# Long convolutions of a Hyena layer: float32 operands in place of hi/lo splits, one matrix table, more buffers and a lag of three

## The chip, the cores and the metric

One NeuronCore of a Trainium2 chip runs the whole program. The metric is the device time of one execution in microseconds (us); the time of a kernel is the median of its runs.

## What is computed

The reference is a small diffusion backbone: two layers, width 1024, 1024 latent tokens (and 256 context tokens). Layer 0 mixes with an RG-LRU, layer 1 with a bidirectional Hyena operator of order 2; a squared-ReLU MLP follows each, a norm ends it. The change touches the two long convolutions of the Hyena operator alone:

```python
def long_conv(u, k_f, bias):
    L = u.shape[1]
    u32 = u.astype(jnp.float32)
    y = jnp.fft.irfft(jnp.fft.rfft(u32, n=2 * L, axis=1) * k_f, n=2 * L, axis=1)[:, :L]
    return (y + u32 * bias).astype(u.dtype)

def hyena_operator(u, p, conv_fn):
    ...
    v, x1, x2 = jnp.split(z, HYENA_ORDER + 1, axis=-1)
    k_f = hyena_filters(L, fw1, fb1, fw2, fb2, fw3, fb3, fw4, freq)
    v = x1 * long_conv(v, k_f[:, 0], skip[0])
    v = x2 * long_conv(v, k_f[:, 1], skip[1])
    return v @ w_out + b_out
```

Each convolution is a product of spectra over 2L = 2048 points. `x1` (in the code X1) and `x2` (the tensor x2d) are gates.

## The kernel before

The kernel computes the transforms as block transforms on TensorE. A convolution order `o` and a half `c` of the 1024 channels are one unit, (0,0), (0,1), (1,0), (1,1). A unit's data is `BIG[u]`, 128 partitions x 16 blocks x 512 channels of float32; block `f` is one group of frequencies. Four functions in `hyena` do the work.

- `s1(u, g)` (L815 to L826): the first half of the forward transform for group g. Two float32 matmuls with `m1` (L822), each evicted by ScalarE into a tile `e` (L824; three buffers), which a DMA scatters into eight partition rows of `BIG[u]` (L826, big<-e).
- `fstep(u, j)` (L936 to L974): one step for frequency block `f = FORD[j]`. A DMA fetches the filter's block `ft` (L940; three buffers), a float32 matmul with `m2f` transforms it (L947), ScalarE copies it to `kk` (L949). BIG's block is split into two float32r tiles: `ah`, a rounded copy on ScalarE (L943), and `al`, the rest (L944), on POOL in odd steps and on DVE in even ones. `mm3` multiplies as three float32r matmuls, hi x hi, lo x hi, hi x lo (L133 to L135), with `m2h` and `m2l`. Four products of 64 partitions each on DVE form the complex product of the spectra, t1 and t2 (L956 to L959), and a sum follows (L968 at the ends of a unit; L970 in the ten middle steps, which are split again into `yh`, L972, and `yl`, L974).
- `bstep(u, j, y)` (L976 to L983): the transform back of block f, by mm3 with `mih`, `mil` in the middle steps and by a float32 matmul with `mif` (L982) in the others; ScalarE evicts it into `BIG[u]` (L983).
- `s2p(u, g)` (L920 to L934): the second half of the way back. Two DMAs gather rows of BIG into tiles `e` (L927, e<-big; five buffers), two float32 matmuls with `md` (L928), then DVE multiplies by the gate X1 (L932) in order 0, or ScalarE copies (L934) in order 1.

The loop runs 64 fsteps, 16 a unit. Bstep i-LAG stands behind fstep i, with LAG 2. Between them stand side items, spread over steps 0 to 12 of unit 0 and LAG+1 to 12 of the others: eight s1 of unit 1 in unit 0; s2p of the unit before, then s1 of the unit after, in units 1 and 2; s2p of unit 2, then four `back` (transposes L999, gate by x2d L1000) in unit 3. So s2p(u-1) and s1(u+1) run beside the steps of u. Unit 3's own s2p come after the loop, inside the output projection. BIG of units 0 and 2 share one buffer, those of 1 and 3 another. PE's instructions keep program order in the loop (`pin`); the framework's scheduler places the others. The DMAs of s1, s2p and fstep are all issued on SyncE (SP). The tables m2h, m2l, mih and mil come over POOL's queue in pieces during unit 0, m2f and mif over SyncE's.

Of the kernel before, what the change touches and what calls it, by code (L numbers as in the profile page):

```python
# [16 lines left out]
P = 128  # L17
# [21 lines left out]
FORD = list(range(1, 9)) + [0] + list(range(9, 16))  # L39
# [7 lines left out]
def tile_block(ctx: ExitStack, tc: tile.TileContext, a, out, dbg=None):  # L47
    nc = tc.nc
# [74 lines left out]
    def pin(ins):  # L123

        if pinned[0]:
            if pinned[0] is not True:
                tc.add_manual_dep(ins.ins, pinned[0], NOSYNC, reason="order")
            pinned[0] = ins.ins.name
        return ins

    def mm3(ps, wh, wl, rh, rl, start, stop):

        first = pin(nc.tensor.matmul(ps, wh, rh, start=start, stop=False))  # L133
        pin(nc.tensor.matmul(ps, wh, rl, start=False, stop=False))  # L134
        pin(nc.tensor.matmul(ps, wl, rh, start=False, stop=stop))  # L135
        return first
# [652 lines left out]
    def hyena(load, xs, close_x, close_w, reopen_x, reopen_w):  # L789
        vst, bst = ExitStack(), ExitStack()  # L790
        units = [(0, 0), (0, 1), (1, 0), (1, 1)]
        cp = [None]
        with ExitStack() as st2:
# [21 lines left out]
            def s1(u, g):  # L815

                o, c = units[u]
                if g == 0 and u != 1:
                    BIG[u] = (cp[0] if u % 2 else xb).tile([P, 16, 512], F32, tag="big", name=nm("big"), bufs=1)
                for m in range(2):  # L820
                    ps = psum()
                    pin(nc.tensor.matmul(ps, m1[:, m], V[c][:, g], start=True, stop=True))  # L822
                    e = bp.tile([P, 512], F32, tag="e", name=nm("e"), bufs=3)
                    nc.scalar.copy(e, ps)  # L824
                    b = prow(2 * g + m)
                    nc.sync.dma_start(BIG[u][b:b + 29:4], e)  # L826
# [63 lines left out]
        with ExitStack() as st:  # L890
            cp[0] = bst.enter_context(tc.tile_pool(name="hd", bufs=1, side="right", reuse_waits="tile"))
            cA = st.enter_context(tc.tile_pool(name="hca", bufs=1, reuse_waits="tile"))
            cpool = st.enter_context(tc.tile_pool(name="hcb", bufs=1, reuse_waits="tile"))
            LAG = 2
            E2 = 5
            BIG[1] = cp[0].tile([P, 16, 512], F32, tag="big", name=nm("big"), bufs=1)
            m2 = {}
            for q in (0, 1, 3, 2):
                m2[q] = [cA.tile([P, 4, P], F32R, name=f"m2{n}{q}") for n in "hl"]

            for tag, dt, n in (("ah", F32R, 2), ("al", F32R, 2), ("kk", F32, 2), ("t1", F32, 2), ("t2", F32, 2), ("y", F32, LAG)):
                cpool.tile([P, 512], dt, tag=tag, name=nm(tag), bufs=n)
            mih = cpool.tile([P, 10, P], F32R, name="mih")
            mil = cpool.tile([P, 10, P], F32R, name="mil")
            mif = cpool.tile([P, 6, P], F32, name="mif")
# [8 lines left out]
            def load_mif(o):
                nc.sync.dma_start(mif[:, o:o + 3], a["mif"][:, o:o + 3])

            def load_mi(o):
                for t, n in ((mih, 0), (mil, 1)):
                    nc.gpsimd.dma_start(t[:, o:o + 5], a["mi"][n, :, o:o + 5])

            def s2p(u, g):
                o, c = units[u]
                po = psum()
                for m in range(2):
                    e = cp[0].tile([P, 512], F32, tag="e2", name=nm("e2"), bufs=E2)
                    b = prow(2 * g + m)
                    nc.sync.dma_start(e, BIG[u][b:b + 29:4])  # L927
                    pin(nc.tensor.matmul(po, md[:, m], e, start=(m == 0), stop=(m == 1)))  # L928
                if o == 0:
                    if g == 0:  # L930
                        V[c] = vtile()
                    nc.vector.tensor_tensor(V[c][:, g], po, X1[c][:, g], op=ALU.mult)  # L932
                else:
                    nc.scalar.copy(V[c][:, g], po)  # L934

            def fstep(u, j):  # L936
                o, c = units[u]
                f = FORD[j]
                ft = cA.tile([P, 512], F32, tag="ft", name=nm("ft"), bufs=3)
                nc.sync.dma_start(ft, fd[u, f])  # L940
                ah = cpool.tile([P, 512], F32R, tag="ah", name=nm("ah"), bufs=2)
                al = cpool.tile([P, 512], F32R, tag="al", name=nm("al"), bufs=2)
                nc.scalar.copy(ah, BIG[u][:, f])  # L943
                (nc.gpsimd if j % 2 else nc.vector).tensor_tensor(al, BIG[u][:, f], ah.bitcast(F32), op=ALU.subtract)  # L944

                pk = psum()
                pin(nc.tensor.matmul(pk, m2f[:, f], ft, start=True, stop=True))  # L947
                kk = cpool.tile([P, 512], F32, tag="kk", name=nm("kk"), bufs=2)
                nc.scalar.copy(kk, pk)  # L949

                ps = psum()
                mm3(ps, m2[j // 4][0][:, j % 4], m2[j // 4][1][:, j % 4], ah, al, True, True)
                t1 = cpool.tile([P, 512], F32, tag="t1", name=nm("t1"), bufs=2)
                t2 = cpool.tile([P, 512], F32, tag="t2", name=nm("t2"), bufs=2)
                lo, up = slice(0, 64), slice(64, 128)
                nc.vector.tensor_tensor(t1[lo], ps[lo], kk[up], op=ALU.mult)  # L956
                nc.vector.tensor_tensor(t1[up], ps[up], kk[up], op=ALU.mult)
                nc.vector.tensor_tensor(t2[lo], ps[up], kk[lo], op=ALU.mult)
                nc.vector.scalar_tensor_tensor(t2[up], ps[lo], -1.0, kk[lo], op0=ALU.mult, op1=ALU.mult)  # L959
                if f == 0:  # L960

                    nc.vector.tensor_copy(t1[64:65], t2[0:1])
                    nc.vector.memset(t2[0:1], 0.0)
                    nc.vector.memset(t2[64:65], 0.0)
                mid = 3 <= j < 13
                y = cpool.tile([P, 512], F32R if mid else F32, tag="y", name=nm("y"), bufs=LAG)
                if not mid:
                    nc.vector.tensor_tensor(y, t1, t2, op=ALU.add)  # L968
                    return y, None
                nc.vector.tensor_tensor(t1, t1, t2, op=ALU.add)  # L970
                yh = cpool.tile([P, 512], F32R, tag="yh", name=nm("yh"), bufs=LAG)
                nc.scalar.copy(yh, t1)  # L972
                yl = y
                (nc.gpsimd if j % 2 else nc.vector).tensor_tensor(yl, t1, yh.bitcast(F32), op=ALU.subtract)  # L974
                return yh, yl

            def bstep(u, j, y):
                ps = psum()
                if y[1] is not None:
                    mm3(ps, mih[:, j - 3], mil[:, j - 3], y[0], y[1], True, True)  # L980
                else:
# [10 lines left out]
            def back(ct):  # L992
# [3 lines left out]
                for g4 in range(2):  # L996
# [227 lines left out]
def _consts():  # L1224
# [164 lines left out]
```

## Time and profile before

| | us |
|---|---|
| median of 3 runs (2871.66 to 2874.5) | 2873.65 |
| the profiled execution, its own time | 2870.54 |
| its span in the trace | 2868.8 |
| PE busy in the span | 2680.0 |
| DVE busy | 1605.5 |
| ACT busy | 1098.6 |
| POOL busy | 245.2 |
| the loop of the block transforms, 1682.68 to 2032.40 | 349.72 |

Busy times are sums over one engine's instructions; engines run beside each other, so they do not add up. The loop begins with the first matmul of L947 and ends with the last eviction at L983. Its frequency steps can be told apart by the matmuls of L947: steps 0, 16, 32, 48 begin at 1682.7, 1749.4, 1837.1 and 1942.5 us, which are the ends of the units below. A float32 matmul leaves two records in the trace. In the rows of windows stand begin and end, the length, the busy time of each engine with its count of records, the granted clock, the busy share of the DMA engines and their rate. PEclk is the granted clock of TensorE as a share of its upper level.

### The profile page before, as it was taken

The page shows a single profiled execution, that of the slowest core. Times are in us where ns is not written, and L with a number is a line of the kernel's source. Part 1 is how long each engine was busy: PE and PEld are TensorE (multiplying, and loading weights), DVE is VectorE, ACT ScalarE, POOL GpSimd, SP SyncE. Part 2 cuts the span into 40 slices and gives each one's busy share as a digit, 9 for nine tenths or more (in the row PEclk, how much of TensorE's full clock was granted, in tenths as well). Part 3 has the DMA queues.
Part 4 walks back from the last instruction along what each step waited for, and adds up shares of the span by engine and source line. Part 5 has one row for each costly group of instructions (what it writes and reads, how often), then busy time and mean ns, then how long its engine had stood idle before and what let it go on. Part 6 is the DMA issues. An engine that isn't in the chain of part 4 may idle for free.

```text
span 2868.8 us, 29759 instructions
## 1 busy us (share of the span) xinstructions
PE 2680.0 (93%) x11298; PEld 2071.4 (72%) x11298; DVE 1605.5 (56%) x2193; ACT 1098.6 (38%) x1670; POOL 245.2 (9%) x154
## 2 busy tenths in 40 slices
PE   6789889999999999999999997778799999999998
PEld 1677777788777777788787763334488888888887
DVE  7666575875555555444833368768576333333336
ACT  6457667542333233322522244444434211122213
POOL 0223432100000000000100021112001000000000
PEclk8799999999999999999999999998899999999999
DMA  8431123344444434322313254455321111111112
GB/s 304 125 111 44 52 66 121 102 145 133 121 114 138 122 114 138 100 68 63 123 52 118 67 159 122 134 159 169 120 87 45 52 52 44 52 44 52 51 46 96
DMA packets 121794, 288.60 MB, mean 101 GB/s; under 512 B 11883, under 2 KB 28269, under 8 KB 121395
## 3 DMA queue, kind: packets, MB, share of 16 engines
q1 hardware_dynamic: 116578, 275.42, 31.6%
q0 software_dynamic: 3344, 9.18, 1.0%
q10 hardware_dynamic: 1728, 2.10, 0.2%
q8 instruction: 89, 1.46, 0.2%
q14 instruction: 55, 0.44, 0.0%
HBM read 215.08 MB, written 37.75 MB: 88 GB/s over the span
## 4 chain that ended last, share of the span: by engine, by line
PE 72%; DVE 11%; DMA 9%; ACT 6%; issue 2%; SPq 0%; POOL 0%; DVEq 0%; ACTq 0%; POOLq 0%
PE ps L152 52%; PE ps L134 4%; PE ps L133 4%; PE ps L135 4%; DMA e<-big 3%; DMA adaw<-in_ada_w_dram 2%; PE ps L396 2%; PE ps L928 1%; DVE xc L485 1%; DMA big<-e 1%; DMA eraw<-in_ada_w_dram 1%; DVE hf L588 1%; PE ps L822 1%; PE ps L947 1%; ACT r L525 1%
## 5 line engine op out<-in xcount | busy, mean ns | idle before, releaser
L152 PE MATMUL ps<-u,whi 128*128 128x512 f32 x2696 | 734.7, 394 | 0.0
L113 ACT CAST whi<-raw 128x1024 fp32r<-128x1024 f32 x206 | 216.3, 1050 | 1113.5 <-PE ps L152 1007.4
L152 PEld LDWEIGHTS ps<-u,whi 128*128 128x128 f32 x2696 | 505.1, 188 | 113.5 <-issue 7.4
L115 DVE TENSOR_TENSOR wlo<-raw,whi 128x1024 fp32r<-128x1024 f32 x206 | 261.9, 1271 | 467.8 <-ACT whi L113 467.0
L152 PE MATMUL ps<-u,wlo 128*128 128x512 f32 x1348 | 418.9, 390 | 0.0
L152 PE MATMUL ps<-hh,whi 128*128 128x512 f32 x896 | 296.7, 409 | 0.0
L152 PEld LDWEIGHTS ps<-u,wlo 128*128 128x128 f32 x1348 | 253.1, 188 | 53.0 <-DVE wlo L115 0.7
L152 PE MATMUL ps<-hh,wlo 128*128 128x512 f32 x896 | 282.1, 390 | 0.0
L152 PE MATMUL ps<-hl,whi 128*128 128x512 f32 x896 | 280.5, 390 | 0.0
L152 PEld LDWEIGHTS ps<-hh,whi 128*128 128x128 f32 x896 | 168.4, 188 | 51.3 <-issue 17.3
L134 PE MATMUL ps<-u,whi 128*128 128x512 f32 (+1 forms) x508 | 195.2, 385 | 3.5 <-POOL u L260 2.9
L133 PE MATMUL ps<-u,whi 128*128 128x512 f32 (+1 forms) x508 | 186.9, 385 | 11.5 <-ACT u L259 11.5
L745 DVE SCALAR_TENSOR_TENSOR big<-ps,mod,big 128x512 f32<-128x512 f32 (+1 forms) x132 | 91.7, 731 | 185.3 <-PE ps L152 177.7
L135 PE MATMUL ps<-u,wlo 128*128 128x512 f32 (+1 forms) x508 | 193.0, 382 | 1.8 <-DVE wlo L115 1.8
L152 PEld LDWEIGHTS ps<-hl,whi 128*128 128x128 f32 x896 | 168.3, 188 | 36.1 <-issue 1.0
L152 PEld LDWEIGHTS ps<-hh,wlo 128*128 128x128 f32 x896 | 168.2, 188 | 34.9
L745 DVE SCALAR_TENSOR_TENSOR x<-ps,mod,x 128x512 f32<-128x512 f32 x128 | 91.3, 746 | 145.1 <-PE ps L152 137.2
L195 DVE SCALAR_TENSOR_TENSOR acc<-adaw,cond,acc 128x512 f32<-128x512 f32 x98 | 73.6, 751 | 93.1 <-DMA adaw<-in_ada_w_dram 92.2
L260 POOL TENSOR_TENSOR u<-nu,u 128x512 fp32r<-128x512 f32 x24 | 33.9, 1413 | 1021.8 <-ACT u L259 1012.6
L133 PEld LDWEIGHTS ps<-u,whi 128*128 128x128 f32 x508 | 97.8, 193 | 29.9 <-ACT u L259 12.2
L134 PEld LDWEIGHTS ps<-u,whi 128*128 128x128 f32 x508 | 97.9, 193 | 25.4 <-POOL u L260 6.0
L135 PEld LDWEIGHTS ps<-u,wlo 128*128 128x128 f32 x508 | 97.4, 192 | 20.1 <-DVE wlo L115 3.0
(242 smaller groups left out, 4051.2 us busy)
## 6 DMA issues: line engine op xcount, KB each, us to landing
raw<-in_mlp_w_dram SPq DMA_DIRECT2D x136, 512.0 KB
adaw<-in_ada_w_dram SPq DMA_DIRECT2D x112, 256.0 KB
fd<-fe SPq DMA_DIRECT2D x64, 256.0 KB
big<-e SPq DMA_DIRECT2D x64, 256.0 KB
ft<-fd SPq DMA_DIRECT2D x64, 256.0 KB
e<-big SPq DMA_DIRECT2D x64, 256.0 KB
eraw<-in_ada_w_dram SPq DMA_DIRECT2D x24, 512.0 KB
raw<-in_hy_w_in_dram SPq DMA_DIRECT2D x24, 512.0 KB
```

The costliest lines, as they stand in the source:

```text
L113: lsplit[0] = nc.scalar.copy(hi, raw)
L115: lsplit[1] = nc.vector.tensor_tensor(lo, raw, hi.bitcast(F32), op=ALU.subtract)
L133: first = pin(nc.tensor.matmul(ps, wh, rh, start=start, stop=False))
L134: pin(nc.tensor.matmul(ps, wh, rl, start=False, stop=False))
L135: pin(nc.tensor.matmul(ps, wl, rh, start=False, stop=stop))
L152: nc.tensor.matmul(pp[c], x, y[c][k], start=first, stop=last)
L195: nc.vector.scalar_tensor_tensor(acc, w, s, acc, op0=ALU.mult, op1=ALU.add)
L260: applied[k % 2] = (nc.vector if k % 2 else nc.gpsimd).tensor_tensor(ul[k], u, uh[k].bitcast(F32), op=ALU.subtract)
L396: nc.tensor.matmul(p2, mf[:, 1 if g == 0 else 0], st.pop(("ht", i)), start=True, stop=True)
L485: eng.scalar_tensor_tensor(ov[:, :, so], zv[:, :, si], vcol("lru_conv_w", 8 * tap_ + dt), ov[:, :, so], op0=ALU.mult, op1=ALU.add)
L525: ins = nc.scalar.activation(*args, **kw)
L745: nc.vector.scalar_tensor_tensor(xs[m][:, cs], ps[:, :n], g2[:, m:m + 1], xs[m][:, cs], op0=ALU.mult, op1=ALU.add)
```

## The change

In the loop all operands are float32, and nothing is split. A step is one matmul for the filter, one for the signal and one back. One table `m2` (4 pieces of 128 x 4 x 192, whose columns 0 to 127 transform the signal and 64 to 191 the filter) and one table `mi` (4 pieces of 128 x 4 x 128) take the place of m2h, m2l, m2f, mih, mil and mif; all pieces come over POOL's queue. The sum y stands on GpSimd in all 64 steps. The DMA big<-e is issued on ScalarE for the units in the loop. Buffers: ft 3 to 8, e of s2p 5 to 6, kk, t1 and t2 2 to 3, y 2 to 4; LAG 2 to 3, so side items of units 1 to 3 begin a step later too. Nothing moves before the loop or after the beginning of the output projection.

```diff
@@ s1
-                    nc.sync.dma_start(BIG[u][b:b + 29:4], e)
+                    (nc.scalar if cp[0] else nc.sync).dma_start(BIG[u][b:b + 29:4], e)
@@ pools and tables
-            LAG = 2
-            E2 = 5
+            LAG = 3
...
+            m2 = [cA.tile([P, 4, 192], F32, name=f"m2{q}") for q in range(4)]
+            mi = [cA.tile([P, 4, P], F32, name=f"mi{q}") for q in range(4)]
+            for tag, n in (("kk", 3), ("t1", 3), ("t2", 3), ("y", LAG + 1)):
+                cpool.tile([P, 512], F32, tag=tag, name=nm(tag), bufs=n)
...
-            nc.sync.dma_start(m2f, a["m2f"])
...
             def load_m2(q):
-                for n in range(2):
-                    nc.gpsimd.dma_start(m2[q][n], a["m2w"][n, :, 4 * q:4 * q + 4])
+                nc.gpsimd.dma_start(m2[q], a["m2"][:, 4 * q:4 * q + 4])
...
+            def load_mi(q):
+                nc.gpsimd.dma_start(mi[q], a["mi"][:, 4 * q:4 * q + 4])
@@ s2p
-                    e = cp[0].tile([P, 512], F32, tag="e2", name=nm("e2"), bufs=E2)
+                    e = cp[0].tile([P, 512], F32, tag="e2", name=nm("e2"), bufs=6)
@@ fstep
-                ft = cA.tile([P, 512], F32, tag="ft", name=nm("ft"), bufs=3)
+                ft = cA.tile([P, 512], F32, tag="ft", name=nm("ft"), bufs=8)
                 nc.sync.dma_start(ft, fd[u, f])
-                ah = cpool.tile([P, 512], F32R, tag="ah", name=nm("ah"), bufs=2)
-                al = cpool.tile([P, 512], F32R, tag="al", name=nm("al"), bufs=2)
-                nc.scalar.copy(ah, BIG[u][:, f])
-                (nc.gpsimd if j % 2 else nc.vector).tensor_tensor(al, BIG[u][:, f], ah.bitcast(F32), op=ALU.subtract)
+                w = m2[j // 4][:, j % 4]
                 pk = psum()
-                pin(nc.tensor.matmul(pk, m2f[:, f], ft, start=True, stop=True))
+                pin(nc.tensor.matmul(pk, w[:, 64:192], ft, start=True, stop=True))
...
-                mm3(ps, m2[j // 4][0][:, j % 4], m2[j // 4][1][:, j % 4], ah, al, True, True)
+                pin(nc.tensor.matmul(ps, w[:, 0:128], BIG[u][:, f], start=True, stop=True))
...
-                mid = 3 <= j < 13
...
-                nc.vector.tensor_tensor(t1, t1, t2, op=ALU.add)
-                yh = cpool.tile([P, 512], F32R, tag="yh", name=nm("yh"), bufs=LAG)
-                nc.scalar.copy(yh, t1)
-                yl = y
-                (nc.gpsimd if j % 2 else nc.vector).tensor_tensor(yl, t1, yh.bitcast(F32), op=ALU.subtract)
-                return yh, yl
+                y = cpool.tile([P, 512], F32, tag="y", name=nm("y"), bufs=LAG + 1)
+                nc.gpsimd.tensor_tensor(y, t1, t2, op=ALU.add)
+                return y
@@ bstep
-                if y[1] is not None:
-                    mm3(ps, mih[:, j - 3], mil[:, j - 3], y[0], y[1], True, True)
-                else:
-                    pin(nc.tensor.matmul(ps, mif[:, j if j < 3 else j - 10], y[0], start=True, stop=True))
+                pin(nc.tensor.matmul(ps, mi[j // 4][:, j % 4], y, start=True, stop=True))
@@ before the loop
             load_m2(0)
-            late = {1: lambda: load_mif(0), 2: lambda: (nc.sync.dma_start(md, a["md"]), load_m2(1)), 3: lambda: load_mi(0),
-                    6: lambda: (load_m2(2), load_mi(5)), 9: lambda: (load_m2(3), load_mif(3))}
+            nc.sync.dma_start(md, a["md"])
+            load_mi(0)
+            late = {1: lambda: load_m2(1), 3: lambda: load_mi(1), 5: lambda: load_m2(2), 7: lambda: load_mi(2),
+                    9: lambda: load_m2(3), 11: lambda: load_mi(3)}
```

In what order the queues stand is seen at three places. SyncE's queue in unit 1, at the beginning of its s2p items, where it issues ft (the filter's blocks) and e (rows of BIG for s2p). Before:

```order
L940 DMA ft_12668<-fd 128x512
L927 DMA e_2436_12649<-big_10982 128x1x512
L927 DMA e_2437_12652<-big_10982 128x1x512
L927 DMA e_2440_12658<-big_10982 128x1x512
L927 DMA e_2441_12661<-big_10982 128x1x512
L927 DMA e_2454_12694<-big_10982 128x1x512
L940 DMA ft_12712<-fd 128x512
L940 DMA ft_12750<-fd 128x512
L927 DMA e_2455_12697<-big_10982 128x1x512
L927 DMA e_2457_12702<-big_10982 128x1x512
L927 DMA e_2458_12705<-big_10982 128x1x512
```

After the change, the same place:

```order
L928 DMA ft_12675<-fd 128x512
L915 DMA e_2390_12479<-big_10982 128x1x512
L915 DMA e_2391_12482<-big_10982 128x1x512
L915 DMA e_2394_12488<-big_10982 128x1x512
L915 DMA e_2395_12491<-big_10982 128x1x512
L915 DMA e_2405_12515<-big_10982 128x1x512
L915 DMA e_2406_12518<-big_10982 128x1x512
L928 DMA ft_12714<-fd 128x512
L928 DMA ft_12753<-fd 128x512
L915 DMA e_2408_12523<-big_10982 128x1x512
L915 DMA e_2409_12526<-big_10982 128x1x512
```

Six tiles e stand ahead of the next ft instead of five, the ft run further ahead of their steps, and no big<-e stands in this queue.

ScalarE's queue in unit 1, where its s1 items begin: e is s1's eviction, kk the filter's, big<-ps the eviction of a bstep, ah and yh the rounded copies. Before:

```order
L824 COPY e_12865<-ps_12863 128x512
L824 COPY e_12870<-ps_12868 128x512
L824 COPY e_12875<-ps_12873 128x512
L824 COPY e_12880<-ps_12878 128x512
L983 COPY big_11985<-ps_12883 128x512
L949 COPY kk_12896<-ps_12894 128x512
L972 CAST yh_12859<-t_2511_12848 128x512
L943 CAST ah_12980<-big_11985 128x512
L824 COPY e_12915<-ps_12913 128x512
L824 COPY e_12920<-ps_12918 128x512
L824 COPY e_12925<-ps_12923 128x512
L824 COPY e_12930<-ps_12928 128x512
```

After the change:

```order
L934 COPY kk_12679<-ps_12677 128x512
L824 COPY e_12693<-ps_12691 128x512
L826 DMA big_12622<-e_12693 8x16x512
L824 COPY e_12698<-ps_12696 128x512
L824 COPY e_12703<-ps_12701 128x512
L826 DMA big_12622<-e_12698 8x16x512
L826 DMA big_12622<-e_12703 8x16x512
L824 COPY e_12708<-ps_12706 128x512
L957 COPY big_11985<-ps_12711 128x512
L826 DMA big_12622<-e_12708 8x16x512
L934 COPY kk_12718<-ps_12716 128x512
L824 COPY e_12732<-ps_12730 128x512
```

The rounded copies are gone; the DMAs of big<-e stand among the copies, each behind the copy of its e, and some of them with the next copy ahead.

TensorE's queue, the last plain steps of unit 0. Before, with L947 the filter, L133 to L135 with ah and al the signal, the same lines with yh and y the block back in a middle step, and L982 the block back in another:

```order
L947 MATMUL ps_12502<-ft_12496,m2f 128x512
L133 MATMUL ps_12506<-ah_12498,m2h_11990 128x512
L134 MATMUL ps_12506<-al_12499,m2h_11990 128x512
L135 MATMUL ps_12506<-ah_12498,m2l_11991 128x512
L133 MATMUL ps_12518<-yh_12461,mih 128x512
L134 MATMUL ps_12518<-y_12459,mih 128x512
L135 MATMUL ps_12518<-yh_12461,mil 128x512
L947 MATMUL ps_12529<-ft_12523,m2f 128x512
L133 MATMUL ps_12533<-ah_12525,m2h_11990 128x512
L134 MATMUL ps_12533<-al_12526,m2h_11990 128x512
L135 MATMUL ps_12533<-ah_12525,m2l_11991 128x512
L982 MATMUL ps_12545<-y_12489,mif 128x512
```

After the change, with L932 the filter, L937 the signal and L956 the block back:

```order
L932 MATMUL ps_12350<-ft_12348,m_11989 128x512
L937 MATMUL ps_12354<-big_10982,m_11989 128x512
L956 MATMUL ps_12364<-y_12295,mi_11992 128x512
L932 MATMUL ps_12369<-ft_12367,m_11989 128x512
L937 MATMUL ps_12373<-big_10982,m_11989 128x512
L956 MATMUL ps_12383<-y_12324,mi_11993 128x512
L932 MATMUL ps_12388<-ft_12386,m_11986 128x512
L937 MATMUL ps_12392<-big_11985,m_11986 128x512
L956 MATMUL ps_12402<-y_12343,mi_11993 128x512
```

The five or seven matmul instructions of a step became three, all of float32, and the block that goes back is one step older.

## Rows read from the trace of the kernel before

**Rows 1.** The page, part 1: busy us of each engine (share of the span, instructions).

```profile
PE 2680.0 (93%) x11298; PEld 2071.4 (72%) x11298; DVE 1605.5 (56%) x2193; ACT 1098.6 (38%) x1670; POOL 245.2 (9%) x154
```

**Rows 2.** Windows by unit, then the loop: PE, PEld, DVE, ACT, POOL busy, PEclk, DMA, GB/s.

```profile
1682.68:1749.30 66.62, 55.23 (x150) 29.19 (x151) 63.00 (x94) 41.08 (x74) 19.33 (x18) 0.95 0.59 177
1749.30:1837.05 87.75, 72.36 (x187) 35.08 (x186) 67.61 (x101) 40.10 (x75) 16.93 (x13) 0.96 0.53 144
1837.05:1942.45 105.40, 79.75 (x187) 37.68 (x186) 74.91 (x110) 41.08 (x75) 17.17 (x14) 0.89 0.53 142
1942.45:2032.40 89.95, 66.72 (x191) 35.07 (x189) 76.40 (x108) 38.64 (x67) 16.63 (x13) 0.90 0.44 132
1682.68:2032.40 349.72, 274.06 (x712) 137.01 (x712) 281.92 (x410) 160.90 (x289) 70.05 (x57) 0.92 0.52 146
```

**Rows 3.** Windows: s2p of unit 1, its s1, s2p of unit 2, the slowest 20 us.

```profile
1760.90:1796.20 35.30, 30.02 (x71) 14.12 (x70) 26.13 (x40) 10.73 (x19) 6.35 (x5) 0.90 0.59 151
1796.20:1829.30 33.10, 29.39 (x82) 14.29 (x80) 23.70 (x36) 19.19 (x37) 6.73 (x5) 1.00 0.50 144
1852.10:1897.90 45.80, 33.12 (x72) 14.81 (x71) 26.45 (x41) 10.82 (x19) 6.34 (x5) 0.85 0.66 165
1860.00:1880.00 20.00, 14.74 (x26) 5.93 (x26) 7.78 (x12) 4.51 (x8) 1.69 (x2) 0.74 0.75 192
```

**Rows 4.** Groups of instructions in the loop: busy us, mean ns, then idle before and releasers.

```profile
L928 PE MATMUL ps<-e,md 128*128 128x512 f32 x96 | 53.9, 669 | 22.7 <-DMA e<-big 22.6
...
L957 DVE TENSOR_TENSOR t<-ps,kk 64x512 f32<-64x512 f32 x64 | 44.4, 694 | 0.9
...
L944 POOL TENSOR_TENSOR al<-big,ah 128x512 fp32r<-128x512 f32 x32 | 41.9, 1311 | 167.3 <-ACT ah L943 163.3 <-DMA ft<-fd 4.0
L943 ACT CAST ah<-big 128x512 fp32r<-128x512 f32 x64 | 40.0, 627 | 11.2 <-PE ps L135 5.0 <-DMA big<-e 4.6
...
L970 DVE TENSOR_TENSOR t<-t,t 128x512 f32<-128x512 f32 x40 | 30.5, 765 | 0.3
L982 PE MATMUL ps<-y,mif 128*128 128x512 f32 x48 | 29.4, 703 | 18.7 <-DVE y L968 17.1 <-ACT e L824 0.8 <-ACT ah L943 0.8
L824 ACT COPY e<-ps 128x512 f32<-128x512 f32 x48 | 27.9, 590 | 27.3 <-DMA big<-e 24.9 <-PE ps L822 2.1
...
L972 ACT CAST yh<-t 128x512 fp32r<-128x512 f32 x40 | 24.8, 622 | 19.5 <-DVE t L970 19.4
L944 DVE TENSOR_TENSOR al<-big,ah 128x512 fp32r<-128x512 f32 x32 | 24.1, 753 | 2.1 <-ACT ah L943 1.5
...
L968 DVE TENSOR_TENSOR y<-t,t 128x512 f32<-128x512 f32 x24 | 16.4, 688 | 0.5
L974 DVE TENSOR_TENSOR y<-t,yh 128x512 fp32r<-128x512 f32 x20 | 14.6, 729 | 6.9 <-ACT yh L972 4.2 <-PE ps L947 2.2
...
L999 PE MATMUL ps<-ident,v 128*128 128x128 f32 x32 | 4.4, 274 | 0.0
```

**Rows 5.** SyncE's queue in the loop, waits: us in total, times, longest.

```profile
SPq L940 <- PE ps L947: 98.4, 36, 8.1
SPq L826 <- ACT e L824: 37.7, 23, 4.0
```

**Rows 6.** The chain, 1795 to 1812 us: start us, length us, what (x records).

```profile
1796.37 0.86 PE ps L947 x2
1797.22 0.23 PE ps L133
...
1797.92 3.43 PE ps L822 x8
...
1807.01 4.40 DMA big<-e
```

**Rows 7.** Instructions on tile e, 1682 to 2040 us: ns min/median/max, first and last start.

```profile
L826 SPq DMA_DIRECT2D big<-e x48: 608/614/660, 1688.3 to 1930.0; - x48
```

**Rows 8.** Instructions of L1217, output at the end: ns min/median/max.

```profile
L1217 ACTq DMA_DIRECT2D out_dram<-o x12: 338/338/374, 2846.4 to 2865.6; - x12
```

More of the change, by code (lines that the diff above doesn't have):

```diff
@@ L893, in hyena @@
             cpool = st.enter_context(tc.tile_pool(name="hcb", bufs=1, reuse_waits="tile"))
-            LAG = 2
-            E2 = 5
+            LAG = 3
             BIG[1] = cp[0].tile([P, 16, 512], F32, tag="big", name=nm("big"), bufs=1)
[L897 to L905, printed above, removed]
+            m2 = [cA.tile([P, 4, 192], F32, name=f"m2{q}") for q in range(4)]
+            mi = [cA.tile([P, 4, P], F32, name=f"mi{q}") for q in range(4)]
+            for tag, n in (("kk", 3), ("t1", 3), ("t2", 3), ("y", LAG + 1)):
+                cpool.tile([P, 512], F32, tag=tag, name=nm(tag), bufs=n)
             md = cp[0].tile([P, 2, P], F32, name="md")
-            m2f = cA.tile([P, 16, P], F32, name="m2f")
-            nc.sync.dma_start(m2f, a["m2f"])
             def load_m2(q):
-                for n in range(2):
-                    nc.gpsimd.dma_start(m2[q][n], a["m2w"][n, :, 4 * q:4 * q + 4])
[L914 to L919, printed above, removed]
+                nc.gpsimd.dma_start(m2[q], a["m2"][:, 4 * q:4 * q + 4])
+            def load_mi(q):
+                nc.gpsimd.dma_start(mi[q], a["mi"][:, 4 * q:4 * q + 4])
             def s2p(u, g):
@@ L938, in fstep @@
                 f = FORD[j]
-                ft = cA.tile([P, 512], F32, tag="ft", name=nm("ft"), bufs=3)
+                ft = cA.tile([P, 512], F32, tag="ft", name=nm("ft"), bufs=8)
                 nc.sync.dma_start(ft, fd[u, f])
-                ah = cpool.tile([P, 512], F32R, tag="ah", name=nm("ah"), bufs=2)
-                al = cpool.tile([P, 512], F32R, tag="al", name=nm("al"), bufs=2)
-                nc.scalar.copy(ah, BIG[u][:, f])
-                (nc.gpsimd if j % 2 else nc.vector).tensor_tensor(al, BIG[u][:, f], ah.bitcast(F32), op=ALU.subtract)
+                w = m2[j // 4][:, j % 4]
                 pk = psum()
-                pin(nc.tensor.matmul(pk, m2f[:, f], ft, start=True, stop=True))
-                kk = cpool.tile([P, 512], F32, tag="kk", name=nm("kk"), bufs=2)
+                pin(nc.tensor.matmul(pk, w[:, 64:192], ft, start=True, stop=True))
+                kk = cpool.tile([P, 512], F32, tag="kk", name=nm("kk"), bufs=3)
                 nc.scalar.copy(kk, pk)
                 ps = psum()
-                mm3(ps, m2[j // 4][0][:, j % 4], m2[j // 4][1][:, j % 4], ah, al, True, True)
-                t1 = cpool.tile([P, 512], F32, tag="t1", name=nm("t1"), bufs=2)
-                t2 = cpool.tile([P, 512], F32, tag="t2", name=nm("t2"), bufs=2)
+                pin(nc.tensor.matmul(ps, w[:, 0:128], BIG[u][:, f], start=True, stop=True))
+                t1 = cpool.tile([P, 512], F32, tag="t1", name=nm("t1"), bufs=3)
+                t2 = cpool.tile([P, 512], F32, tag="t2", name=nm("t2"), bufs=3)
                 lo, up = slice(0, 64), slice(64, 128)
@@ L964, in fstep @@
                     nc.vector.memset(t2[64:65], 0.0)
-                mid = 3 <= j < 13
[L966 to L969, printed above, removed]
-                nc.vector.tensor_tensor(t1, t1, t2, op=ALU.add)
-                yh = cpool.tile([P, 512], F32R, tag="yh", name=nm("yh"), bufs=LAG)
-                nc.scalar.copy(yh, t1)
-                yl = y
-                (nc.gpsimd if j % 2 else nc.vector).tensor_tensor(yl, t1, yh.bitcast(F32), op=ALU.subtract)
-                return yh, yl
+                y = cpool.tile([P, 512], F32, tag="y", name=nm("y"), bufs=LAG + 1)
+                nc.gpsimd.tensor_tensor(y, t1, t2, op=ALU.add)
+                return y
             def bstep(u, j, y):
                 ps = psum()
-                if y[1] is not None:
-                    mm3(ps, mih[:, j - 3], mil[:, j - 3], y[0], y[1], True, True)
-                else:
-                    pin(nc.tensor.matmul(ps, mif[:, j if j < 3 else j - 10], y[0], start=True, stop=True))
+                pin(nc.tensor.matmul(ps, mi[j // 4][:, j % 4], y, start=True, stop=True))
                 nc.scalar.copy(BIG[u][:, FORD[j]], ps)
@@ L1281, in _consts @@
     mf[1, 0, 16, 0, :] = c1_[0]
-    def two(m):
-        hi = (m.view(np.int32) & np.int32(-4096)).view(np.float32)
-        return np.stack([hi, m - hi], 0)
     def lay(m, w=P):
@@ L1303, in _consts @@
     decay = np.ascontiguousarray(np.broadcast_to(-deltas, (P, D)))
-    return dict(m1=lay(m1), md=lay(md), mf=lay(mf), m2w=two(lay(m2[FORD][:, :, :P])), m2f=lay(m2[:, :, 64:]), mi=two(lay(mi[FORD[3:13]])), mif=lay(mi[FORD[:3] + FORD[13:]]), pos=pos2, tpos=tpos, decay=decay)
+    return dict(m1=lay(m1), md=lay(md), mf=lay(mf), m2=lay(m2[FORD], 192), mi=lay(mi[FORD]), pos=pos2, tpos=tpos, decay=decay)
 def _layout(i):
```

## The prediction

> **What bounds the kernel now.** Start with the page: TensorE (PE) is busy 93% of the span [rows 1]. That is a mean. Outside the block transforms its matmuls stand shoulder to shoulder and the change touches nothing, so the loop must be read alone: 1682.68 to 2032.40 us, 349.72 us, PE busy 274.06, VectorE (DVE) 281.92, ScalarE (ACT) 160.90, GpSimd (POOL) 70.05, DMA share 0.52 [rows 2]. No engine is full; the limit alternates. In unit 0 DVE is busy 63.00 of 66.62 us [rows 2]. Units 1 to 3 take 87.75, 105.40 and 89.95 us with neither PE nor DVE full [rows 2]. There two stretches must be told apart. While the s2p items run (e comes back from BIG, matmul, DVE or ACT), five or six frequency steps take 35.30 and 45.80 us; PE is busy 30.02 and 33.12 of it, at a granted clock of 0.90 and 0.85 of the upper level, 2.4 GHz [rows 3]. While the s1 items run, 33.10 us, PE 29.39 [rows 3].
>
> What do those stretches wait for? The engines' rows: PE idles 22.7 us before L928 and almost all of it is for DMA e<-big; ACT idles 27.3 before the e copy, 24.9 of it for DMA big<-e [rows 4]. The queue that issues these transfers says why they are late: SyncE stood 98.4 us in 36 waits at L940 (next ft) for the PE matmul that frees one of three ft buffers, 37.7 at L826 for ACT's e [rows 5]; e<-big stands behind both in program order.
>
> **The sum, part by part.** What PE does is priced from the chain at full clock: one float32 matmul (two records, L947) 0.86 us, eight records of L822 3.43, a split product 3 x 0.23 = 0.69 (L133, and the same for L134 and L135) [rows 6].
> - *PE.* 64 products and 40 middle back transforms go from 0.69 to 0.86: 104 x 0.17 = **+17.7 us** of PE work. After: 3 x 64 in steps, 96 in s1 and s2p, 288 x 0.86 = 247.7, and 4.4 for back's transposes (L999 [rows 4]): 252 us, the floor of the loop if nothing ever waits.
> - *DVE.* Leave: al 24.1, sums 30.5 and 16.4, yl 14.6 = **85.6 us** [rows 4]. Stay: four products of some 690 ns a step (L957 694; 64 x 2.77 = 177), s2p's and back's work. DVE comes to some 197 us and is full nowhere but in plain steps.
> - *ACT.* Leave 64 ah (40.0) and 40 yh (24.8) [rows 4]; come 48 issues of big<-e. One cost 614 ns on SyncE [rows 7]; ACT's nearest issue is that of the output, 338 [rows 8]. 48 of them are 16 to 29 us; I take 25 (the same transfer, so nearer the first). They lie on the ACT queue behind the e copy, with kk and the evictions behind them.
> - *POOL.* al and yl leave, 64 sums come, at 1311 ns (the same shape and two SBUF operands, L944) 84 us [rows 4]. A step of 2.9 us covers 1.3. Lag three gives a sum two whole steps before its back transform asks; before, L982 stood 17.1 us for DVE's sum [rows 4]. Should the cover fail, each step would grow by the 0.6 us by which POOL is slower.
> - *Tables.* One m2 and one mi, 2.5 MB by their tile shapes, take the place of 4.7. The first step's matmuls now both wait for m2's first quarter, 384 KB, where the first matmul of before used m2f, which had been loaded earlier on SyncE; I put 1.5 us there, between 0 and 4.40, the landing time of a 256 KB transfer [rows 6].
>
> Plain step, without a side item: PE 3 x 0.86 = 2.58, DVE 4 x 0.69 + gaps = 2.86; DVE sets it. Unit 0 shows what DVE's old five or six instructions cost: 66.62/16 = 4.2 us a step [rows 2].
>
> *Unit 0:* 8 steps carry one s1 (2.58 + 2 x 0.86 = 4.30 PE) and 8 do not. Bound 34.4 + 22.9 = 57.3; with the start and the e buffers (three, filled again only when big<-e has landed, 4.40 us [rows 6]) 60.5. **Gain 6.**
>
> *Units 1 and 2:* four steps carry two s2p each: PE 2.58 + 4 x 0.86 = 6.02. Four tiles e a step then come from DMA; before, 16 took about 35 us with five buffers, that is 2.2 each, with ft's waits in the queue. With the waits gone (eight ft buffers) and six in flight I take 1.5 to 1.6, so 6.3 us a step, 25 in all, against 35.30. Four or five steps carry two s1: PE again 6.02, but three e buffers recirculate in (0.59 + 4.40 + issue 0.3)/3 = 1.76 us, so 7 us for four e; 28.5 in all, against 33.10. Seven plain steps: 20.0. Unit 1 is 73.5 (before 87.75), **gain 14**; unit 2 has 2 MB of v<-x2d in the queue of its s2p items, 5 to 6 us more: 79.5 (105.40), **gain 26**.
>
> *Unit 3:* s2p 25 and some 2 of lead, four steps with back items 17, seven plain steps, 20, end of the pipe and big<-xd's start 8: 72 (89.95), **gain 18**.
>
> Sum of gains 64. From this I take 3 for half-clock stretches: the loop's mean clock is 0.92 [rows 2], and a loop with less idle should lose fewer, not more, but PE's float32 work lasts twice as long there. And 1 for the end, where the last sum now takes POOL's 1.3 us and not DVE's 0.69. Net **-60**. The profiled execution took 2870.54, so 2810.5; the median of the runs, 2873.65, is 3 us above it, and against that my figure is **2813 us**.
>
> One more thing on the queue that changes. What the move of big<-e takes off SyncE is 48 x 0.61 = 29 us of issuing and the 37.7 us of standing for e [rows 5, 7]; my s1 stretch stays held by three buffers and 4.40 us, with 28.5 us. If the other queue also made the transfer itself quicker, say 3 us, four e would take 4 x 1.3 = 5.2 us, PE's 6.02 would set the step, and three units would gain some 8 us more. The Trainium skill, in Trainium Kernel Development and Optimization, section Key Constraints, says that DMAs of all issuing queues run on the same 16 DMA engines, and that several queues save issue time only. By that rule the 8 us do not come; no row here has such a transfer on another queue.
>
> **Rivals.**
> 1. *Transfers keep their pace.* If e<-big is slow because of the DMA engines and not because SyncE stood at ft, the s2p stretches stay near 35 and 46 us and the s1 stretch near 33; only the plain steps and unit 0 gain. For: DMA share 0.59 and 0.66 in the s2p windows [rows 3]. Against: 98.4 us of waits ahead of them in the queue [rows 5]. Price: of the 60, 10 in each of units 1 and 3, 15 in unit 2, and 2 x 4.5 for s1 fall away: gain 16, 2858.
> 2. *PE alone sets the pace.* Buffers and lag cover everything: 252 plus about 12 for start, end and half clock: loop 264, gain 86, 2787. DVE's 2.86 against PE's 2.58 in some 30 plain steps (8 us) speaks against the very end.
> 3. *Half clock (the slower side).* Matmul work at full clock is 252 us. If 35 us of waiting stay, the loop is no shorter than 349.7 once 252/c = 315, a mean clock c of 0.80; the loop now has 0.92, an s2p stretch 0.85 [rows 2, 3]. At 0.74 throughout, the level of the slowest 20 us [rows 3], 252/0.74 + 35 = 375: 2899. Float32 throughout is what makes the clock dear: every wait in an s2p item that drops the clock then doubles 6.02 us of work. The Trainium skill, in TensorE: Matmul & The Clock Gate, section HAM oscillation, tells of a kernel whose matmul bursts fall back to the low clock at each DMA wait; the 0.85 stretch agrees in kind. Against: the s1 stretch has 1.00 [rows 3].
> 4. *ACT chains.* The change does not do what its queue move says: an e copy that waits for its buffer holds kk, the eviction and now the next big<-e itself, all on ACT. Then s1 stretches take 8 us a step instead of 7, three units, 2 x 4.5 + 4: 13 us less gain, 2825.
> 5. *POOL's sums slow DVE's products.* Sums on DVE took 765 ns in the middle steps, while POOL worked, and 688 at the ends of a unit, where it did not [rows 4]. If that ratio, 1.11, falls on the products, a plain step grows to 3.15, 30 of them by 9 us, and the start of the DVE-heavy unit 0 with them: 12 us, 2824. Against: L957, a product, has 694 in the same loop. GPSIMD Engine Reference, section 8 Key points, in the Trainium skill, says that GpSimd shares its SBUF interfaces with VectorE and contends with instructions that have two SBUF inputs; its section 4.1 would keep an add of two tiles on VectorE, as about twice as fast. The trace agrees with both (1311 against 688). A product here has one SBUF input, so by the first the 12 us do not come; by the second, with the sums left on DVE, 0.69 more in each of 30 plain steps would cost 21.
>
> **How the numbers follow.** Forecast as summed 0.47 (2798 to 2828 by the bounds: e<-big 1.3 to 1.9 us each, 48 x 0.3 to either side; issue 16 to 29; start 0 to 4); rival 2 0.16; rival 4 0.14; rival 1 0.12; rival 5 0.08; rival 3 0.03. The range that holds 8 in 10 takes in 4, 5 and the upper part of 2: **2788 to 2842**. What a measurement can tell from no change is 0.2%, 5.7 us; only rival 3 ends above it, and 0.02 is for rival 1 with a low clock on top: faster 0.95, same 0.02, slower 0.03.
>
> **What would show it.** Right: per step one pair at each of the three matmul lines and no split line in the loop; DVE's four product lines unchanged near 690 ns and its busy time near 200; plain steps of 2.8 to 3.0 us; the 98.4 us of ft waits on SyncE gone; POOL near 84 us, with no PE wait for y beyond unit ends; s2p stretches of 25 to 28 us. Wrong: L956's counterpart on PE waiting for POOL's y; products well above 700 ns while POOL adds (sharing of SBUF); s2p stretches still near 35 us with DMA e<-big as releaser (rival 1); granted clock under 0.85 over the loop (rival 3); ACT's e copy with more than the 24.9 us before (rival 4).

## The result and the profile after

The changed kernel takes 2836.32 us in the median (2834.56 to 2838.23, four runs), the kernel before 2873.03: a ratio of 0.9873, 95% interval 0.9859 to 0.9888, faster by 36.7 us. The profiled execution is that of 2838.23 us, with a span of 2836.4. Of the 32.4 us between the two spans, 32.0 are the loop's: 317.73 us now, 349.72 before [rows 2].

The page of the changed kernel, part 1, answers to [rows 1]:

```profile
PE 2682.9 (95%) x11194; PEld 2046.7 (72%) x11194; DVE 1524.7 (54%) x2077; ACT 1044.6 (37%) x1566; POOL 256.7 (9%) x162
```

Windows of the changed kernel by unit, then the loop, with the columns of [rows 2]; units begin at the steps of L932:

```profile
1684.10:1741.66 57.56, 54.62 (x125) 23.41 (x123) 44.22 (x66) 26.51 (x48) 19.71 (x18) 0.97 0.68 218
1741.66:1826.27 84.61, 74.19 (x162) 29.65 (x160) 50.01 (x75) 27.55 (x48) 20.27 (x16) 0.98 0.52 149
1826.27:1920.65 94.38, 77.36 (x162) 30.45 (x161) 51.13 (x76) 27.55 (x48) 20.27 (x16) 0.93 0.58 156
1920.65:2001.83 81.18, 68.24 (x167) 28.48 (x165) 57.15 (x81) 25.80 (x44) 22.85 (x18) 0.94 0.47 139
1684.10:2001.83 317.73, 274.41 (x610) 112.00 (x608) 202.52 (x295) 107.40 (x188) 83.11 (x68) 0.95 0.56 161
```

PE is busy as long as before (274.41 against 274.06). The dearer float32 products are in it, and a higher granted clock, 0.95 against 0.92, goes the other way; what each of the two weighs was not separated. What left is time in which PE stood idle: 75.7 us before, 43.3 now.

Windows of the changed kernel by stretch: s2p of unit 1, its s1, s2p of units 2 and 3, then four plain steps with no side item, 16 to 19:

```profile
1752.00:1787.30 35.30, 28.11 (x57) 10.36 (x56) 20.34 (x30) 4.69 (x8) 7.60 (x6) 0.95 0.56 153
1787.30:1821.00 33.70, 30.51 (x69) 12.31 (x67) 15.12 (x24) 15.34 (x27) 5.07 (x4) 1.00 0.52 154
1836.60:1881.30 44.70, 31.22 (x57) 11.16 (x56) 21.21 (x31) 4.69 (x8) 8.19 (x7) 0.85 0.69 168
1930.90:1970.40 39.50, 32.76 (x70) 12.97 (x69) 21.82 (x34) 11.72 (x20) 9.26 (x8) 0.96 0.60 154
...
1741.70:1752.00 10.30, 10.30 (x26) 4.56 (x25) 10.03 (x16) 4.69 (x8) 5.07 (x4) 1.00 0.34 104
```

Set beside [rows 3] this says where the gain is not: the s2p stretch of unit 1 takes 35.30 us as before, that of unit 2 44.70 (45.80), though each now carries four steps and not five; the s1 stretch takes 33.70 (33.10), with six steps in both; unit 3's s2p, 39.50, has a DMA share of 0.60. And where it is: a plain step takes 2.58 us, PE's three matmuls with nothing between them. Before, the three plain steps at the same place, 16 to 18, took 3.87 us each, and DVE was busy in 11.35 of their 11.60 us:

```profile
1749.30:1760.90 11.60, 7.74 (x22) 3.82 (x21) 11.35 (x18) 5.45 (x10) 2.56 (x2) 1.00 0.36 104
```

Groups of instructions in the changed kernel's loop, columns as in [rows 4], and a wait of SyncE's queue, as in [rows 5]:

```profile
L951 POOL TENSOR_TENSOR y<-t,t 128x512 f32<-128x512 f32 x64 | 81.2, 1268 | 231.2 <-DVE t L944 187.8 <-DVE t L948 28.7 <-PE ps L932 8.4
L956 PE MATMUL ps<-y,mi 128*128 128x512 f32 x128 | 71.0, 638 | 6.4 <-POOL y L951 3.4 <-ACT e L824 3.0
...
L916 PE MATMUL ps<-e,md 128*128 128x512 f32 x96 | 55.2, 677 | 27.4 <-DMA e<-big 26.6 <-DVE v L920 0.7
...
L942 DVE TENSOR_TENSOR t<-ps,kk 64x512 f32<-64x512 f32 x64 | 44.4, 694 | 0.9
...
L824 ACT COPY e<-ps 128x512 f32<-128x512 f32 x48 | 28.1, 586 | 49.9 <-DMA big<-e 35.5 <-PE ps L822 11.7 <-DMA ft<-fd 1.4
```

```profile
SPq L928 <- PE ps L932: 144.5, 47, 8.0
```

PE still waits 26.6 us for DMA e<-big (22.6 before), ACT 35.5 for DMA big<-e (24.9). SyncE's waits for a free ft have not gone but grown, to 144.5 us.

### The profile page after: what moved, and what is told of

Its sections match the earlier page's. It is cut to its first block, busy times and chain, and to the rows that moved or that the text cites. A ratio compares the mean times of both kernels' runs of the same rounds, so it can differ in the third digit from the quotient of the medians.

```text
span 2836.4 us, 29311 instructions
## 1 busy us (share of the span) xinstructions
PE 2682.9 (95%) x11194; PEld 2046.7 (72%) x11194; DVE 1524.7 (54%) x2077; ACT 1044.6 (37%) x1566; POOL 256.7 (9%) x162
## 5 line engine op out<-in xcount | busy, mean ns | idle before, releaser
L133 PE MATMUL ps<-u,whi 128*128 128x512 f32 (+1 forms) x508 | 187.2, 385 | 11.5 <-ACT u L259 11.5
L135 PE MATMUL ps<-u,wlo 128*128 128x512 f32 (+1 forms) x508 | 193.1, 382 | 1.8 <-DVE wlo L115 1.8
L195 DVE SCALAR_TENSOR_TENSOR acc<-adaw,cond,acc 128x512 f32<-128x512 f32 x98 | 73.5, 750 | 92.1 <-DMA adaw<-in_ada_w_dram 90.7
L133 PEld LDWEIGHTS ps<-u,whi 128*128 128x128 f32 x508 | 98.0, 194 | 30.1 <-ACT u L259 12.2
L135 PEld LDWEIGHTS ps<-u,wlo 128*128 128x128 f32 x508 | 97.5, 192 | 20.2 <-DVE wlo L115 3.0
```

What stands on the lines that cost most here:

```text
L195: nc.vector.scalar_tensor_tensor(acc, w, s, acc, op0=ALU.mult, op1=ALU.add)
```

## The experiments

Theory **H**: the transfers between e and BIG are slow in themselves. Each has eight partition rows of BIG on one side and gets half of the 16 DMA engines. The traces agree: the DMA share is 0.50 to 0.60 in these stretches, before [rows 3] and after, and 0.66 and 0.69 only in unit 2's s2p, where the v<-x2d loads run too. Counting the packets in progress every 0.05 us in unit 1's s2p stretch, the commonest number is 8 (about 330 of 706 moments). Which engine took a packet is not in the traces. The main rival: what stands ahead of the transfers in SyncE's queue, as the prediction had it. The Trainium skill, DMA: Bandwidth & Descriptors, section Why a DMA increments its semaphore by 16 and not by 1, says that a transfer runs on the largest number of engines, up to 16, that divides the slowest dimension on both of its sides: 8 for 8 rows against 128. The 8 packets in progress agree.

**w16, 16 rows to a tile.** Rows of BIG are renumbered and the columns of m1 and the rows of md permuted with them, so that one tile e is 16 rows by 8 blocks. Bytes and arithmetic are unchanged.

```diff
 def prow(g):
-    return 32 * (g >> 2) + (g & 3)
+    return 32 * (g >> 2) + (g >> 1 & 1) + 2 * (g & 1)
@@ s1 and s2p
-                    b = prow(2 * g + m)
-                    (nc.scalar if cp[0] else nc.sync).dma_start(BIG[u][b:b + 29:4], e)
+                    b = prow(2 * g)
+                    (nc.scalar if cp[0] else nc.sync).dma_start(BIG[u][b:b + 31:2, 8 * m:8 * m + 8], e)
...
-                    b = prow(2 * g + m)
-                    nc.sync.dma_start(e, BIG[u][b:b + 29:4])
+                    b = prow(2 * g)
+                    nc.sync.dma_start(e, BIG[u][b:b + 31:2, 8 * m:8 * m + 8])
@@ tables
-    gm = 4 * (p >> 5) + (p & 3)
+    gm = 4 * (p >> 5) + 2 * (p & 1) + (p >> 1 & 1)
...
+    m1 = m1.reshape(2, P, 8, 2, 8).transpose(3, 1, 2, 0, 4)
+    md = md.reshape(2, 8, 2, 8, P).transpose(2, 1, 0, 3, 4)
```

> The changed kernel with the rows of BIG renumbered, so that a tile e holds 16 partition rows of BIG by 8 blocks instead of 8 rows by 16 blocks; bytes, number of transfers, queues, buffers and all arithmetic stay. Theory H (half the DMA engines): e<-big and big<-e move at about 150 GB/s with a DMA share of 0.5 to 0.6 whatever the queue, because a transfer with 8 rows on one side runs on 8 of the 16 engines; with 16 rows the s2p stretches fall from 35.3, 44.7 and 39.5 us to 26 to 30 each, the s1 stretches from 33.7 to about 30, and the time by 30 to 45 us to some 2795 to 2805. Rival Q (each transfer's own latency and the number in flight set the pace): no change, within 5 us of 2836.

2797.69 us (2795.1 to 2801.22), 38.6 less than the changed kernel; against before 0.9745 (0.9728 to 0.9761). Windows of w16: s2p of unit 1, its s1, s2p of unit 2, the loop:

```profile
1751.10:1776.20 25.10, 24.49 (x57) 10.39 (x56) 20.00 (x30) 4.68 (x8) 7.34 (x6) 1.00 0.87 205
1776.20:1806.10 29.90, 29.43 (x69) 12.50 (x68) 15.26 (x24) 14.31 (x26) 5.35 (x5) 1.00 0.74 173
1822.00:1854.80 32.80, 26.67 (x57) 10.95 (x58) 21.58 (x32) 4.68 (x8) 8.67 (x7) 0.90 0.83 219
1684.00:1960.10 276.10, 258.21 (x610) 111.30 (x608) 202.06 (x295) 106.68 (x188) 83.14 (x68) 0.98 0.70 186
```

The s2p stretch of unit 1 fell from 35.30 to 25.10 us, the DMA share rose from 0.56 to 0.87, and the clock to 1.00. The DMA digits of the two kernels' s2p stretches (tenths of the engines busy in 40 slices; first the changed kernel, 1754 to 1786, then w16, 1751 to 1776) show the plateau at five and its end:

```profile
DMA  5554599955554558945555555974555555569510
```

```profile
DMA  9999999999899999998998999999999899994000
```

In w16 the commonest number of packets in progress is 16 (about 227 of 503 moments). PE's wait at L916 for DMA e<-big is left with 6.1 us of the 26.6:

```profile
L916 PE MATMUL ps<-e,md 128*128 128x512 f32 x96 | 46.4, 617 | 6.7 <-DMA e<-big 6.1 <-PE ps L937 0.5
```

That a renumbering alone, with every queue and buffer left in place, took this away shows that the shape of the transfer set the pace; the rival falls. Unit 2's s2p took 32.80, above the 26 to 30 expected; one wait for e<-big of 5.4 us stands in it.

**pooldma, engines or ports.** Eight rows could also be slow because eight rows of SBUF can't be read faster. So the changed kernel's own 8-row transfers were put on GpSimd's queue.

```diff
-                    nc.sync.dma_start(e, BIG[u][b:b + 29:4])
+                    nc.gpsimd.dma_start(e, BIG[u][b:b + 29:4])
```

> The changed kernel with e<-big of s2p (8 rows by 16 blocks, as in the change) issued on GpSimd's queue instead of SyncE's. It tells two causes of the slow transfer apart. Engines (a transfer of 8 rows gets 8 engines; on GpSimd's queue the skill lets consecutive transfers begin on other engines in turn): s2p stretches fall below 32 us each in unit 1 unless the sums on GpSimd wait behind the issues, the DMA share in them rises well above 0.6. Ports (eight partition rows of SBUF can't be read faster): the stretches stay at 35 us or more and the share at 0.55 to 0.6.

2830.66 us (2827.69 to 2835.18). Windows of pooldma: s2p of unit 1, that stretch without its first step, s2p of unit 2, the first step of that:

```profile
1754.50:1783.90 29.40, 26.17 (x58) 11.13 (x57) 20.12 (x30) 4.69 (x8) 16.49 (x22) 0.94 0.83 186
1765.80:1783.90 18.10, 18.10 (x44) 8.05 (x43) 12.11 (x19) 3.52 (x6) 7.43 (x10) 1.00 0.78 170
1832.80:1878.10 45.30, 31.33 (x58) 11.60 (x57) 21.59 (x32) 4.69 (x8) 17.81 (x23) 0.81 0.95 166
1832.80:1854.20 21.40, 11.59 (x16) 3.56 (x15) 9.18 (x14) 1.17 (x2) 10.54 (x14) 0.64 0.98 202
```

The same rows now run three steps at PE's own pace (18.10 of 18.10 us) with a DMA share of 0.78, so it was not the eight rows that held the changed kernel to a share of 0.56. The same section of the Trainium skill, in DMA: Bandwidth & Descriptors, says that GpSimd's queue takes the engines for such transfers in turn, SyncE's always the lowest-numbered. The share of 0.83 in unit 1 agrees. The packets on GpSimd's queue are of 4 KB where SyncE's are of 2, so the choice of engines is not all that differs. Unit 2 stayed at 45.30, with all of PE's 14.0 us of idle time put down to DMA e<-big and none to a sum. 21.40 us of it are the first step: the four v<-x2d loads, which now have no e ahead of them on SyncE, run beside the e there, the DMA share is 0.98 and the granted clock 0.64. The time as a whole gained little; what the sums lose behind the issues on GpSimd's queue was not tried by itself.

**before16, the renumbering without the change.** The same edit in the kernel before.

> The kernel before the change, with the 16-row numbering alone; splits, buffers and lag as before. Theory H: the s2p stretches of before, 35.3 and 45.8 us, shrink by 6 to 10 us each, the time by 20 to 30 us to about 2845 to 2852; its limit is then DVE and ACT. Rival: before is held by SyncE's ft waits with three buffers, and gains under 10 us.

2841.41 us (2839.86 to 2842.38), 0.9894 (0.988 to 0.9909): 28.8 us less than before and better than expected, though SyncE's three ft buffers, the splits and the lag are as they were. L928, a wait of SyncE's queue and the loop of before16:

```profile
L928 PE MATMUL ps<-e,md 128*128 128x512 f32 x96 | 44.9, 601 | 2.9 <-DMA e<-big 2.9
```

```profile
SPq L940 <- PE ps L947: 87.7, 35, 8.4
```

```profile
1682.40:2001.20 318.80, 263.95 (x712) 135.15 (x712) 282.63 (x409) 160.74 (x289) 70.96 (x57) 0.94 0.63 161
```

Before's wait for e<-big, 22.6 us at L928 [rows 4], is down to 2.9, while SyncE still stands 87.7 us for a free ft (98.4 before [rows 5]): in the kernel before, too, it was the transfer and not the queue ahead of it.

**ft3.** Three ft buffers in the changed kernel (`bufs=8` to `bufs=3`).

> The changed kernel with three ft buffers as before, not eight. The prediction's step (SyncE's waits for a free ft hold e<-big back): the s2p stretches grow again and the time by 10 to 20 us. Theory H: they are paced by the transfers themselves, 35, 45 and 40 us as they are, and the time stays within 4 us of 2836.

2835.05 us (2834.1 to 2835.92). No difference, with 152.3 us of SyncE's waits for a free ft against 144.5; the prediction's step falls.

**nobuf.** All buffers and the lag as before: ft 3, e of s2p 5, kk, t1, t2 and y 2, LAG 2.

> The changed kernel with the buffers and the lag of before: ft 3, e of s2p 5, kk, t1, t2 and y 2, LAG 2. What is left is the arithmetic: float32 operands, no splits, sums on GpSimd. If the buffers and the lag carry the plain steps: these grow from 2.58 to 3.3 or more, and the time by 10 to 20 us against 2836. If the absent splits alone carry them: within 5 us of 2836.

2835.84 us (2835.58 to 2837.01), 0.9875 (0.9859 to 0.9892). The whole gain of the change stands without one of its buffers and without its lag. What is left is the float32 arithmetic without splits, the sums on GpSimd, which dvesum prices at 12.7 us, and big<-e on ScalarE, which spdma shows to bring nothing. That the rest is the splits' absence follows by taking these away; no run puts the splits back alone.

**w16nb.** The same small buffers with the 16-row numbering.

> The 16-row numbering with the buffers and the lag of before (ft 3, e 5, kk, t1, t2 and y 2, LAG 2). With slow transfers buffers and lag were worth nothing (2835.8 against 2836.3). If they are of use only where the transfers keep up: 2805 to 2815, against 2797.7 with them. If they are of no use at all: 2795 to 2800.

2792.98 us (2790.7 to 2794.17), lower by 4.7 than w16 with the large ones, though its loop in the trace is no shorter (279.4 us; w16 276.1). They are of no use that shows there either. In the traces the difference lies behind the loop, 829.8 us to the end against 834.9; why it is shorter there stays open.

**dvesum.** The sums on VectorE (`nc.gpsimd` to `nc.vector` at L951).

> The changed kernel with the sum y on VectorE instead of GpSimd in all 64 steps. If VectorE's time in plain steps and in unit 0 counts: a plain step takes 3.5 us instead of 2.58, unit 0 some 62 us instead of 57.6, and the time grows by 10 to 20 us. Rival: the waits for transfers in the s2p and s1 stretches absorb it, and only unit 0 grows, by about 4 us.

2848.98 us (2845.29 to 2852.71), 12.7 more. Plain steps 17 to 19 take 3.55 us: DVE has four products and a sum of 690 ns in each. Unit 0 grew by only 0.9 us, where 4 had been expected. PE's back transform shows the new wait in the loop of dvesum:

```profile
L956 PE MATMUL ps<-y,mi 128*128 128x512 f32 x128 | 72.9, 655 | 17.8 <-DVE y L951 13.3 <-ACT e L824 3.1 <-DVE t L944 1.0
...
L951 DVE TENSOR_TENSOR y<-t,t 128x512 f32<-128x512 f32 x64 | 43.7, 690 | 1.6
```

**spdma and w16sp.** big<-e on SyncE again, alone and with the 16 rows.

> The changed kernel with big<-e issued on SyncE again. Theory H: the same eight DMA engines carry it, so the transfer is as slow; s1 stretches stay at 33 to 34 us and the time within 5 us of 2836, to either side. Rival (the queue counts, as the change has it): e waits behind ft on SyncE and the time grows by over 10 us.

> The 16-row numbering together with big<-e back on SyncE. With big<-e on SyncE alone the time was 2830.4, 6 us under the changed kernel. If that gain is ScalarE's (its queue no longer holds kk and the evictions behind an issue), it comes again: 2790 to 2794. If it came from the slow transfers (e waiting less), it is gone with them: 2797 to 2799.

2830.36 us (2826.75 to 2834.94) and 2796.41 (2792.86 to 2797.01). ScalarE's queue brought nothing. Alone, the move back is 6 us faster than the changed kernel, a little more than the 5 expected of H, with intervals that overlap (0.9842 to 0.9874 against 0.9859 to 0.9888); with quick transfers 1.3 us remain. Whether the move costs those 6 us stays open.

**best1, a faster version.** w16sp with four ft buffers and the v<-x2d loads behind the ft of step 50.

```diff
...
+                    if i == 51:
+                        with tc.issue_after(fts[50].ins):
+                            for ct in range(4):
+                                gate(ct, v[:, 2 * ct:2 * ct + 2].rearrange("p a b -> p (a b)"))
```

> w16sp with four ft buffers, so that fewer transfers crowd the loop's start, and with the 2 MB of v<-x2d queued behind the ft of step 50, out of unit 2's s2p stretch, where one wait for e<-big of 5.4 us stood. Expected: 2 to 3 us at the start and 7 us in unit 2, 2783 to 2788. Rival: the 2 MB cost the same where they now stand, in unit 3, and only the start gains: 2791 to 2795.

2786.33 us (2784.06 to 2789.14), 0.9704 (0.9689 to 0.9718): 50 us under the changed kernel, 84 under before. Windows of best1: s2p of units 1 and 2, the loop:

```profile
1744.20:1768.90 24.70, 24.54 (x57) 10.41 (x56) 20.05 (x30) 4.69 (x8) 7.32 (x6) 1.00 0.87 209
1813.60:1839.30 25.70, 24.25 (x57) 10.48 (x56) 19.77 (x30) 4.69 (x8) 7.36 (x6) 1.00 0.84 201
1679.50:1944.70 265.20, 254.75 (x610) 111.66 (x609) 202.10 (x295) 106.62 (x188) 83.36 (x68) 0.99 0.72 192
```

PE is busy 254.75 of 265.20 us: the loop is now close to what its matmuls cost. Against w16sp, unit 0 shrank from 57.3 to 54.4 us, which the ft buffers alone can have done, and unit 2 from 79.2 to 70.4, where the v<-x2d loads had stood.

## Why the prediction was right or wrong

The direction held, with 36.7 us of gain where 60 were forecast. That the time lies in the range is partly luck: transfers that stayed slow were set off in part by plain steps and a unit 0 that came out shorter than forecast. The nearest single value is that of rival 4, 11 us below, which has another reason. (By their own prices of 13 and 12 us, rivals 4 and 5 come to 2826 and 2825.)

*The step that failed* is s2p's: "With the waits gone (eight ft buffers) and six in flight I take 1.5 to 1.6". Sixteen tiles took 35.30 us, 2.2 each, as before. The 98.4 us of SyncE's waits [rows 5] were real and harmless: ft3 and nobuf change nothing, and the waits grew while the kernel got faster. The forecast blamed the queue and gave no row for a quicker transfer; the DMA share of 0.59, which it put down for rival 1, was a plateau near half the engines. With 16 rows the stretch takes 25.10 us, the 25 that it had counted on. The s1 stretch, 28.5 forecast for four or five steps, took 33.70 for six, two of them at PE's 6.01 us; w16 takes 29.90 for the same six, so the transfers cost 3.8 there. Against the forecast's unit figures the kernel took 11 us more in unit 1 (84.61 against 73.5), 15 in unit 2 (94.38 against 79.5) and 9 in unit 3 (81.18 against 72). With the transfers made quick, w16's units take 56.8, 70.6, 77.7 and 71.0 us, near the 60.5, 73.5, 79.5 and 72 of the sum.

*Rival 1* had the mechanism, with a chance of 0.12, and the wrong price, 2858: plain steps were taken at 2.86 us and unit 0 at 60.5; they measured 2.58 and 57.56. A plain step is set by PE, not DVE: DVE's four products need 2.83, but PE runs ahead by the lag and DVE catches up in the next stretch of waiting. (In nobuf, with a lag of two, plain steps ahead of an s2p stretch do take 2.83, and the time is the same: what they lose is waited out at the next transfer anyway.)

*Rival 2*, the loop at PE's pace with 264 us and 2787, is what best1 reaches, 265.20 and 2786.33, once another limit than the one named there is lifted. *Rival 3*: the clock rose. *Rival 4*: ACT's wait for big<-e did grow, 24.9 to 35.5 us, at a cost that spdma puts at 6 us or nothing. *Rival 5*: the products take 694 ns as they did (L942 against L957 [rows 4]) with 81.2 us of sums on POOL beside them; no price. Its ratio of 1.11 came from a mean: of the 40 sums at L970 three took 1753 to 1768 ns, each beside a subtraction on POOL, and the median is 685.

*Sizes that held:* DVE's busy time of 202.52 (197 forecast), POOL's 81.2 (84), a sum of 1268 ns on POOL (1311). Unit 0 gained 9.1 where 6 was forecast.

*Sizes off or right by luck:* the loop starts 1.4 us later (1.5 forecast), but no matmul waits there for the new table; the work ahead of the loop ended later, and the runs' loops start between 1679.5 us (best1) and 1685.8 (pooldma). An issue of big<-e on ScalarE took 624 ns, 48 of them 30 us (16 to 29). The 5 to 6 us for the v<-x2d loads, for which the forecast has no row, came out as 7 to 9: in w16 unit 2 takes 7.1 us more than unit 1, and with the loads moved, among other things, it shrank by 8.8 in best1.

The Trainium skill, GPSIMD Engine Reference, section 4.1 Engine selection, would keep the sums on VectorE. Here that costs 12.7 us, where the forecast priced it at 21; at 0.69 us that is what some 18 steps lose, not 30.

So the change gained by taking busy time, 79 us off DVE and 53 off ACT in the loop, out of the chain between a step's matmuls, which made plain steps shorter. It gained no more, since the s2p stretches, 119.5 of the loop's 317.73 us, and in part the s1 stretches wait for 8-row transfers that it left as they were.

## What to carry to other kernels

A DMA share that sits at 0.5 for long need not mean that there is room: look at how many rows the transfer has on its narrower side before the queue, the buffers or the issuing engine are blamed. A wait in a queue costs only if the work behind it would otherwise have run; test it by making the resource scarce (ft3) as readily as by adding more. Two limits in series hide each other: the renumbering alone was worth 28.8 us and the arithmetic with small buffers 34, but both together 80 (w16nb, 2792.98, against 2873.47 for before on the same chip).

## What was not expected

Transfers of 256 KB between 8 and 128 partition rows of SBUF, issued on SyncE, kept 8 packets in progress: 153 GB/s at a share of 0.56 in the s2p stretch of unit 1, some ft loads among them, against 205 GB/s and 0.87 for the same bytes as 16 rows. Twice the packets in progress did not give twice the rate: a packet of 2 KB there took 96 ns in the median in the changed kernel and 162 in w16. What limits the transfers then, no run here tells. VectorE's products from PSUM showed no slowing by GpSimd's sums (694 ns at L942 and, before, at L957).
